# A hybrid RWKV-7/gMLP layer on one core: the inverse's substitution given out in 15 portions, its turning pinned, and the transposing of token rows made a stream of its own

## The chip, the cores and the metric

The kernel runs as one program on one core of a Trainium2 chip. The metric is the time of an execution in microseconds (us) on the device. The engines named below are TensorE (PE, matrix products), VectorE (DVE), ScalarE (ACT), GpSimd (POOL) and SyncE (SP, which here only issues DMA transfers). Each engine works through its own instructions strictly in the order in which they stand in the program.

## The reference

One layer on 576 tokens (64 of a running stream, 512 of a new one), 1024 channels, everything in fp32. What matters here:

```python
p   = rms_norm(x) @ w_in                 # columns: RWKV r|k|v|lora, gMLP u|v, gate_A, gate_B
o_a = rwkv7(p)                           # per token t, 16 heads of 64:
#   sa = S a_t ; S = S * w_t + sa b_t^T + v_t k_t^T ; y_t = S r_t       (a = -kk, b = kk * a_rate)
#   out = (group_norm(y) + sum(r * k * r_k) * v) * g                   ("bonus" is the second term)
o_b = gmlp(p)
m   = sigmoid(gate_A) * (o_a @ w_proj_a) + sigmoid(gate_B) * (o_b @ w_proj_b)
x   = x + rms_norm(m @ w_o)
x   = x + rms_norm((silu(f @ w_gate) * (f @ w_up)) @ w_down)           # f = rms_norm(x)
```

## The kernel before, in words

**Layout.** Activations lie with channels on the 128 partitions and tokens along the free axis (128 x 576, worked in two halves of 288). A weight block of 128 columns is loaded (`raw`, two buffers), split into a rounded high part on ACT (`whi`, line 303) and the rest on POOL (`wlo`, line 306), and used in three products per k-step (line 287, helper `mmul`). A block of `w_in` is 2 halves x 8 k-steps x 3 = 48 products `pj` of 128x288.

**The middle stage** (about 100 to 640 us of the span) is the time mixing. It goes over 8 pairs of heads (`hp_`), each in the chunked form: 9 chunks of 64 tokens. Its parts are Python generators ("streams") that record instructions:

- `elementwise`: the decay products `z` (four, line 287), `sg`, the running sum `L` (a DVE scan, line 671), the exponentials `EL` and `sg<-L` (lines 675 and 677), the square `q<-k` (line 685) and its column sums `n` on PE, `AR` and `BK`, the in-chunk products `am` and from them `AB` and `AK`. It then goes on in the same generator to transpose token rows (`tb`, `tr`, `tv` on PE; `At`, `Kt`, `Vt` are the copies) and to form `WV`, and last to the bonus (`bo` on PE, then `bonus` on DVE). Event `A` is set after `am`, `tb` and `values` on the way, `elem` at the end, and only after `elem` does the next pair's `elementwise` begin.
- `inverse`: inverts the 64x64 triangular matrices. Its 16x16 diagonal blocks go through DRAM: eight transfers `d_inv<-AB` (line 748), one load `M<-d_inv`, then 15 substitution steps of two DVE instructions each (`Xt<-X,M`, line 853, and `X<-X,Xt`, line 856), then `d_inv<-X` and eight transfers `IV<-d_inv` (line 861). `turn()` is a DVE transposition `IT<-IV` (line 864) that waits for them; PE products `m`, `mp`, `mu` then put the blocks together, with a second `turn()` between.
- `batch`: products `d`, `e`, `c` for all chunks; nine DVE instructions (lines 955 and 956) write `TD` and `AR` from `e`, and two ACT copies write `C` from `c` (line 959); then the products `y`.
- `chain`: the recurrence over chunks. A first pair of products `pc` is followed by two DVE additions `S` and `So` (line 994), then six more times one product `pc` and one addition; each `pc` needs the addition before it. Then `py`.
- `finish`: group norm, `to`, `g`, output to DRAM (`d_oa`).

**What sets the order.** `Weave.run` keeps a planned clock: a stream yields either a planned delay (table `LAT`) or an event with a delay, and while all streams wait, `pj` products of the next weight block are put in. The order in which PE's instructions are recorded is the order in which PE runs them (`manual_schedule`). For the other engines a scheduler orders the instructions of each engine by its own idea of when their inputs are ready, preferring what was recorded earlier; `keep_in_program_order(ins)` pins an instruction behind whatever was recorded last on its engine before it. Before the change the first `Xt` of each inverse is pinned, and all 30 substitution instructions are recorded at one planned instant. The blocks for `r`, `k` and `v` of the next pair are taken out of PSUM only after event `elem` of the pair before (`project(..., after=...)`).

**After the middle stage** come the output products `pa`, `pb`, `po` and the feed-forward `fg`/`pd`, which the diff does not touch. Between the last pair's chain and the first `pa` stand the products `gv`.

## Time and profile before

| | |
|---|---|
| median of 3 runs | 1273.09 us (1272.32 to 1274.91) |
| the profiled execution | 1264.63 us, span 1262.8 us |
| mean granted TensorE clock in it | 0.966 |
| PE busy | 1200.6 us of the span (95%) |
| DVE / ACT / POOL busy | 43% / 37% / 49% |

All views of the profile come from this one execution. Times in a view count from the start of its span. A matmul group's "idle before" is the time that PE stood still just ahead of its instructions, with the instruction that ended that wait. PEclk is the granted share of PE's full clock in a stretch. Since PE is busy for 95% of the span, the time can change mainly through what PE waits for and through its clock.

### The profile page before, as it was taken

The page shows a single profiled execution, that of the slowest core. Times are in us where ns is not written, and L with a number is a line of the kernel's source. Part 1 is how long each engine was busy: PE and PEld are TensorE (multiplying, and loading weights), DVE is VectorE, ACT ScalarE, POOL GpSimd, SP SyncE. Part 2 cuts the span into 40 slices and gives each one's busy share as a digit, 9 for nine tenths or more (in the row PEclk, how much of TensorE's full clock was granted, in tenths as well). Part 3 has the DMA queues.
Part 4 walks back from the last instruction along what each step waited for, and adds up shares of the span by engine and source line. Part 5 has one row for each costly group of instructions (what it writes and reads, how often), then busy time and mean ns, then how long its engine had stood idle before and what let it go on. Part 6 is the DMA issues. An engine that isn't in the chain of part 4 may idle for free.

```text
span 1262.8 us, 29911 instructions
## 1 busy us (share of the span) xinstructions
PE 1200.6 (95%) x12926; PEld 1166.8 (92%) x12926; DVE 539.3 (43%) x1081; ACT 464.4 (37%) x889; POOL 614.8 (49%) x484
## 2 busy tenths in 40 slices
PE   7999999989999899989999999989999999999997
PEld 6989889888898889879999999989999999999996
DVE  5755545663655356533452542464333333300003
ACT  5545253533544353524351223452222222222220
POOL 6656244542445254522353654366565656543442
PEclk9999898998998989889999999989999999999998
DMA  5233221322132212223354543222222222243222
GB/s 180 82 101 98 62 79 50 96 71 67 47 90 66 71 54 73 76 65 90 117 187 131 191 146 111 69 108 87 86 86 92 85 85 84 80 155 92 76 76 75
DMA packets 68276, 118.05 MB, mean 93 GB/s; under 512 B 30832, under 2 KB 36208, under 8 KB 68144
## 3 DMA queue, kind: packets, MB, share of 16 engines
q1 hardware_dynamic: 68000, 116.06, 30.0%
q8 instruction: 101, 1.65, 0.5%
q14 instruction: 31, 0.25, 0.1%
q10 hardware_dynamic: 144, 0.08, 0.0%
HBM read 99.83 MB, written 16.28 MB: 92 GB/s over the span
## 4 chain that ended last, share of the span: by engine, by line
PE 70%; DVE 11%; ACT 5%; issue 5%; DMA 4%; SPq 3%; POOL 2%; DVEq 0%; ACTq 0%; POOLq 0%
PE fg L287 20%; PE po L287 14%; PE pj L287 11%; PE gv L287 5%; PE pb L287 4%; PE pa L287 3%; SPq L861 2%; DVE X L856 1%; DVE Xt L853 1%; POOL wlo L306 1%; PE fp L287 1%; PE z L287 1%; SPq L748 1%; PE n L287 1%; PE am L287 1%
## 5 line engine op out<-in xcount | busy, mean ns | idle before, releaser
L306 POOL TENSOR_TENSOR wlo<-raw,whi 128x512 fp32r<-128x512 f32 (+1 forms) x288 | 397.0, 1400 | 408.7 <-ACT whi L303 377.4
L303 ACT ACTIVATE whi<-raw 128x1024 fp32r<-128x1024 f32 x144 | 150.1, 1046 | 271.6 <-PE fg L287 168.4
L1274 DVE TENSOR_TENSOR rs<-rs,nsq 128x288 f32<-128x288 f32 (+2 forms) x12 | 9.1, 755 | 105.8 <-ACT nsq L1273 105.8
L1342 DVE TENSOR_TENSOR ft<-ft,fg 128x288 f32<-128x288 f32 x40 | 16.4, 451 | 65.1 <-PE fg L287 63.6
L1336 DVE TENSOR_TENSOR fg<-fg,rs 128x288 f32<-128x288 f32 x40 | 16.5, 453 | 60.1 <-PE fg L287 60.0
L789 POOL TENSOR_TENSOR AR<-eye,eC 128x576 f32<-128x576 f32 x8 | 9.4, 1177 | 63.8 <-PE tr L291 63.8
L853 DVE TENSOR_TENSOR Xt<-X,M 80x15 f32<-80x15 f32 (+7 forms) x120 | 31.0, 258 | 20.1 <-DMA M<-d_inv 16.6
L864 DVE STREAM_TRANSPOSE IT<-IV 128x640 f32<-128x640 f32 x16 | 13.5, 845 | 55.0 <-DMA IV<-d_inv 32.0
L1339 DVE SCALAR_TENSOR_TENSOR ft<-ft,fg 128x576 f32<-128x576 f32 (+1 forms) x24 | 28.6, 1190 | 19.0 <-ACT ft L1338 19.0
L1340 POOL TENSOR_TENSOR ft<-ft,rs 128x576 f32<-128x576 f32 (+1 forms) x24 | 31.6, 1319 | 7.1 <-DVE ft L1339 7.1
L994 DVE TENSOR_TENSOR S<-pc,C 128x64 f32<-128x64 f32 x48 | 10.5, 219 | 55.5 <-PE pc L287 55.5
L856 DVE TENSOR_TENSOR X<-X,Xt 80x15 f32<-80x15 f32 (+7 forms) x120 | 32.0, 266 | 3.5
L287 PE MATMUL pc<-S,TD 128*128 128x64 f32 x112 | 21.6, 278 | 9.9 <-DVE So L994 9.9
L287 PEld LDWEIGHTS pc<-S,TD 128*128 128x128 f32 x112 | 19.6, 210 | 11.4 <-DVE So L994 10.8
L431 ACT ACTIVATE st<-pj 128x288 f32<-128x288 f32 x30 | 12.2, 407 | 48.0 <-PE pj L287 47.4
L287 PE MATMUL pj<-h0h,whi 128*128 128x288 f32 x88 | 29.5, 336 | 0.0
L287 PE MATMUL pj<-h2h,whi 128*128 128x288 f32 x88 | 29.1, 331 | 0.0
L287 PE MATMUL pj<-h1h,whi 128*128 128x288 f32 x88 | 29.1, 331 | 0.0
L287 PE MATMUL pj<-h7h,whi 128*128 128x288 f32 x88 | 28.4, 323 | 0.0
L287 PE MATMUL pj<-h3h,whi 128*128 128x288 f32 x88 | 28.4, 323 | 0.0
L287 PE MATMUL pj<-h4h,whi 128*128 128x288 f32 x88 | 28.3, 322 | 0.0
L287 PE MATMUL pj<-h5h,whi 128*128 128x288 f32 x88 | 28.2, 320 | 0.0
(1200 smaller groups left out, 4323.2 us busy)
## 6 DMA issues: line engine op xcount, KB each, us to landing
raw<-in_w_in SPq DMA_DIRECT2D x50, 512.0 KB, 3.7
raw<-in_w_gate SPq DMA_DIRECT2D x22, 512.0 KB, 3.6
raw<-in_w_up SPq DMA_DIRECT2D x22, 512.0 KB, 3.6
raw<-in_w_down SPq DMA_DIRECT2D x16, 512.0 KB, 3.5
raw<-in_w_gv SPq DMA_DIRECT2D x8, 512.0 KB, 3.7
raw<-in_w_proj_a SPq DMA_DIRECT2D x8, 512.0 KB, 4.0
raw<-in_w_proj_b SPq DMA_DIRECT2D x8, 512.0 KB, 3.7
raw<-in_w_o SPq DMA_DIRECT2D x8, 512.0 KB, 3.6
```

Source lines behind the costliest of these rows:

```text
L287: return pe.matmul(out, lhsT, rhs, **kw)
L303: keep(act.activation(hi[:, :cols], raw[:, :cols], ACT.Copy))
L306: keep(pool.tensor_tensor(lo[:, c0:c1], raw[:, c0:c1], f(hi[:, c0:c1]), ALU.subtract))
L748: sp.dma_start(di[0, h, b].rearrange("u s t -> s u t"), AB[r0_:r0_ + SB].rearrange("p j h t -> p (j h) t")[:, :, SB * b:SB * b + SB])
L853: ins = dve.tensor_tensor(t3, X[:, 0:r, s:s + 1].broadcast_to([NU, r, w]), M[:, s:s + 1, s + 1:SB].broadcast_to([NU, r, w]), ALU.mult)
L856: dve.tensor_tensor(X[:, 0:r, s + 1:SB], X[:, 0:r, s + 1:SB], t3, ALU.add)
L861: sp.dma_start(IV[r0_:r0_ + SB, :, SB * b:SB * b + SB], di[1, h, b].rearrange("u s t -> s u t"))
L864: turn = lambda: dve.transpose(IT.rearrange("p c t -> p (c t)"), IV.rearrange("p c t -> p (c t)"))
L1336: keep(dve.tensor_tensor(g[:, HS[h]], pg, rs2[:, HS[h]], ALU.mult))
L1339: keep(dve.scalar_tensor_tensor(t[:, ts], t[:, ts], 1.0, g[:, ts], ALU.add, ALU.mult))
L1340: pool.tensor_tensor(t[:, ts], t[:, ts], rs2[:, ts], ALU.mult)
L1342: dve.tensor_tensor(t[:, HS[h]], t[:, HS[h]], pu, ALU.mult)
```

## The change

1. The substitution's 15 steps are recorded one by one, 0.75 us of planned time apart (`yield LAT["X"]`), where they were recorded at one instant. Only the first `Xt` is pinned, as before.
2. The first `turn()` of each inverse is pinned behind what is recorded on DVE before it. Its planned delays change (`M` 6.5 to 9.0, `U` 23.0 to 11.0).
3. The transposing of token rows and `WV` leave `elementwise` for a stream `turns` of their own, which starts at event `A`. `elementwise` goes straight from `am` to the bonus, so `elem` is set earlier, and the next pair's `z` follow at once. `lora_w` moves to just after `A`. A new wait keeps `elementwise` behind the transposing of the pair before (`tb`), and the `v` block now also waits for `values` of the pair before.
4. `n2` goes from 6.8 to 8.2 in the plan, with own values for the first two pairs.

No instruction is added or removed on any engine; the arithmetic is the same.

```diff
-    "z0": 5.4, ... "n2": 6.8, ... "bo0": 3.5, "bo": 0.4,
+    "z0": 5.4, ... "n2": 8.2, ... "bo0": 3.5, "v": 2.2, "bo": 0.4,
...
-    "M": 6.5, "U": 23.0, ...
+    "M": 9.0, "X": 0.75, "U": 11.0, ...
...
-        after = ("elem", p_ - 1) if p_ > 0 else None
+        after = [("elem", p_ - 1)] + [("values", p_ - 1)] * (name == "v") if p_ > 0 else []
...
 def elementwise(E):
...
         if hp_ > 1:
             yield (("chain", hp_ - 2), 0.0)
+        if hp_ > 0:
+            yield (("tb", hp_ - 1), 0.0)
...
         clk.signal("A", hp_)
+        if hp_ + 1 < NPAIR:
+            lora[hp_ + 1] = lora_w(lraw)
+        if hp_ > 1:
+            yield (("oa", hp_ - 2), 0.0)
+        rk = q2
...            # the bonus, as it stood at the end before
+        yield LAT["bo0"]
+        yield (("v", hp_), LAT["v"])
...
+        clk.signal("elem", hp_)
+
+    def turns(E):
...            # tb, tr, AR<-eye, tv, WV as they stood in elementwise
         clk.signal("values", hp_)
...
 def inverse(E):
...
-        with tc.high_priority(UPR):
-            for s in range(0, SB - 1):
...
+        for s in range(0, SB - 1):
...
             dve.tensor_tensor(X[:, 0:r, s + 1:SB], X[:, 0:r, s + 1:SB], t3, ALU.add)
+            yield LAT["X"]
...
-        turn()
+        tc.keep_in_program_order(turn())
...
+    def turn_all():
+        for p_ in range(NPAIR):
+            yield (("A", p_), 0.0)
+            yield from turns(EV[p_])
```

On DVE, at the chain of the third pair, this is the order before. `TD` and `AR` belong to that pair, `Xt`, `X` and `IT` to the inverse of the fourth, `S` and `So` are the chain's additions:

```order
L853 TENSOR_TENSOR Xt<-X,M 80x15
L955 TENSOR_TENSOR TD<-e,AR 64x4x64 x2
L856 TENSOR_TENSOR X<-X,Xt 80x15
L956 TENSOR_TENSOR AR<-e,AR 128x4x64
L955 TENSOR_TENSOR TD<-e,AR 64x4x64 x2
L956 TENSOR_TENSOR AR<-e,AR 128x4x64
L955 TENSOR_TENSOR TD<-c,AR 64x64 x2
L956 TENSOR_TENSOR AR<-c,AR 128x64
L864 STREAM_TRANSPOSE IT<-IV 128x640
L994 TENSOR_TENSOR S<-pc,C 128x64
L994 TENSOR_TENSOR So<-pc,C 128x64
```

The 30 instructions of the substitution stand ahead of `TD` here (all but one), and the transposition that waits for the DMA stands ahead of the chain's first additions. The order at the same chain in the changed kernel:

```order
L862 TENSOR_TENSOR Xt<-X,M 80x55
L865 TENSOR_TENSOR X<-X,Xt 80x11x5
L862 TENSOR_TENSOR Xt<-X,M 80x48
L1004 TENSOR_TENSOR S<-pc,C 128x64
L1004 TENSOR_TENSOR So<-pc,C 128x64
L865 TENSOR_TENSOR X<-X,Xt 80x12x4
L862 TENSOR_TENSOR Xt<-X,M 80x39
L865 TENSOR_TENSOR X<-X,Xt 80x13x3
L862 TENSOR_TENSOR Xt<-X,M 80x28
```

The transposition is gone from this place (it stands further down, behind the next pair's `k`), all nine `TD`/`AR` instructions now come before the substitution, and 23 of its 30 instructions stand between them and `S`, seven behind `So`.

On ACT, ahead of the fifth pair's square `q<-k` (for which the products `n` wait), the order before:

```order
L667 ACTIVATE sg<-z,half 128x288 x2
L669 ACTIVATE sg<-sg,chalf 128x576
L667 ACTIVATE ta<-z,half 128x288
L897 ACTIVATE PT<-mp 32x320 x2
L667 ACTIVATE ta<-z,half 128x288
L675 ACTIVATE EL<-L 128x9x64
L677 ACTIVATE sg<-L 128x576
L1036 ACTIVATE oo<-to,vec 128x448
L687 ACTIVATE aq<-ta,nkk 128x576
L485 ACTIVATE shc<-pj 128x1
L486 ACTIVATE q<-pj,vec 128x288
L1036 ACTIVATE oo<-to,vec 128x128
```

and in the changed kernel:

```order
L487 ACTIVATE q<-first 128x2
L843 ACTIVATE WV<-wv 128x512
L844 ACTIVATE WV<-wv 128x128
L484 ACTIVATE shc<-pj 128x1
L485 ACTIVATE q<-pj,vec 128x288
L1031 ACTIVATE gq<-Y 128x640
```

The square comes right behind the last row of each. What waits for the `z` products and the scan `L` stood just ahead of it and is now some 150 `pj` products earlier on PE: between the last `z` and `n` of pairs 2 to 8 stood 30, 12, 33, 12, 27, 15 and 27 products, and now stand 147, 162, 144, 141, 165, 162 and 144.

## The prediction

> **What bounds the kernel now.** I read the page's head first, then the same busy times by stage, then PE's waits.

> ```profile
> span 1262.8 us, 29911 instructions
> PE 1200.6 (95%) x12926; PEld 1166.8 (92%) x12926; DVE 539.3 (43%) x1081; ACT 464.4 (37%) x889; POOL 614.8 (49%) x484
> ```

> ```profile
> 0.00:100.00 100.00, 86.55 (x678) 83.80 (x680) 66.78 (x98) 53.80 (x107) 62.12 (x62) 0.98 0.38 120
> 100.00:640.00 540.00, 504.65 (x7673) 479.15 (x7670) 272.37 (x648) 229.98 (x519) 227.70 (x175) 0.94 0.26 78
> 640.00:1263.00 623.00, 609.41 (x4583) 603.85 (x4581) 200.11 (x336) 180.58 (x264) 325.02 (x248) 0.99 0.33 103
> ```

> PE is the bound. In the middle stage it stands still for 540 - 504.65 = 35.35 us, and its clock is 0.94 there (first figure after POOL's). The change touches this stage alone. Both losses have places. The waits:

> ```profile
> PE n L287 <- ACT q L685: 13.6, 7, 3.1
> PE pc L287 <- DVE So L994: 9.9, 3, 4.0
> PE pc L287 <- ACT C L959: 8.8, 4, 3.5
> PE z L287 <- DVE bonus L834: 3.8, 3, 1.5
> ```

> These are almost all of it (the longest wait for `q`, 3.1 us, belongs to the first pair, ahead of 100 us; small ones make up 2.3 us in sum). The clock, by windows laid on its slow spells:

> ```profile
> 148.80:159.00 10.20, 9.51 (x107) 9.17 (x108) 1.42 (x5) 1.66 (x5) 0.00 (x0) 0.50 0.30 71
> 326.30:329.70 3.40, 3.40 (x16) 3.40 (x15) 2.67 (x7) 0.95 (x2) 2.47 (x2) 0.50 0.01 2
> 558.40:565.20 6.80, 5.71 (x24) 5.71 (x25) 1.48 (x5) 0.00 (x0) 0.00 (x0) 0.50 0.17 61
> sum 64.60, PE 59.29 PEld 57.18 DVE 20.54 ACT 11.78 POOL 16.36; mean PE 6.59 PEld 6.35 DVE 2.28 ACT 1.31 POOL 1.82
> ```

> Nine spells, 64.6 us, at half clock: worth 32.3 us. So the stage loses about 35 + 32 = 67 us, and that is all there is to win.

> **The change, part by part.**

> *The wait of `n`.* The fifth pair before:

> ```profile
> 317.17 0.30 PE L287 MATMUL z<-dwr,lwh 128*128 128x288 f32 x1
> 319.06 2.19 DVE L671 TENSOR_TENSOR_SCAN L<-rmask,sg 128x576 f32<-128x576 f32 x1 [1.88 <-ACT sg L669]
> 321.29 0.69 ACT L675 ACTIVATE EL<-L 128x576 f32<-128x576 f32 x1
> 324.59 0.78 ACT L685 ACTIVATE q<-k,vec 128x576 f32<-128x576 f32 x1
> 325.42 1.53 PE L287 MATMUL n<-cst,q 128*128 128x2 f32 x10 [2.06 <-ACT q L685]
> ```

> The second `z` leads to the scan, the scan to `EL`, and in ACT's order the square `q` stands behind these. 8.25 us pass from that `z` to `n`, with 15 `pj` products and a few small ones between the last `z` and `n`. The change puts 141 to 165 `pj` there, at least 141 x 0.13 us = 18 us. The wait goes for pairs 2 to 8: 13.6 - 3.1 = 10.5 us. What is late next is `k` alone, and it has 8.2 us of plan where its copies, DVE step and square take about 2.5 us. The first pair's `n` stands where it stood; I leave its 3.1 us.

> *The wait of `z`* for `bonus` is for a PSUM bank. `bo` and `bonus` move ahead of `TD` on DVE, with nothing that waits for a DMA before them. I count the 3.8 us as gone.

> *The transposition.* The third pair's chain before:

> ```profile
> 281.60 0.23 DVE L956 TENSOR_TENSOR AR<-c,AR 128x64 f32<-128x64 f32 x1
> 288.60 0.84 DVE L864 STREAM_TRANSPOSE IT<-IV 128x640 f32<-128x640 f32 x1 [6.77 <-DMA X<-in_cst]
> 289.37 0.18 DVE L994 TENSOR_TENSOR S<-pc,C 128x64 f32<-128x64 f32 x1
> 282.41 0.69 PE L287 MATMUL pc<-C,TD 128*128 128x64 f32 x2 [3.51 <-ACT C L959]
> 289.74 0.69 PE L287 MATMUL pc<-S,TD 128*128 128x64 f32 x2 [2.32 <-DVE So L994]
> ```

> DVE stands idle for 6.77 us in front of a transposition whose DMA has not landed, and the addition queued behind it holds PE's second `pc` for 2.32 us. Ahead of that the burst of 30 had held `TD`, and so `C` and the first `pc`, for 3.51 us. With the new order both reasons go in the first, third, fifth and seventh chains: 9.9 + 8.8 = 18.7 us.

> *What comes instead.* At seven of the eight chains 11 to 23 substitution instructions now stand between `TD` and the first `S`, and up to 13 before the next. In five chains the scan `L` of the next pair stands among them, in two ahead of `TD`. PE's second `pc` waits for all of it. The price is bounded by

> ```profile
> L853 DVE TENSOR_TENSOR Xt<-X,M 80x15 f32<-80x15 f32 (+7 forms) x120 | 31.0, 258 | 20.1 <-DMA M<-d_inv 16.6
> L856 DVE TENSOR_TENSOR X<-X,Xt 80x15 f32<-80x15 f32 (+7 forms) x120 | 32.0, 266 | 3.5
> ```

> ```profile
> 274.09 0.22 DVE L853 TENSOR_TENSOR Xt<-X,M 80x60 f32<-80x60 f32 x1
> 274.34 1.17 DVE L856 TENSOR_TENSOR X<-X,Xt 80x60 f32<-80x60 f32 x1
> 274.17 2.51 POOL L306 TENSOR_TENSOR wlo<-raw,whi 128x512 fp32r<-128x512 f32 x2 [6.23 <-ACT whi L303]
> L671 DVE TENSOR_TENSOR_SCAN L<-rmask,sg x8: 1345/2185/2460, 67.1 to 514.2; 128x576 f32<-128x576 f32 x8
> ```

> An undisturbed one takes 0.22 us, 0.24 with the gap behind it; one that meets POOL's `wlo` 1.17. The mean, 0.26 + 0.03, is 0.29 us. The scan takes 1.35 to 2.46 us. How much time PE gives is seen at the last chain, which has no substitution beside it:

> ```profile
> 600.87 1.10 PE L287 MATMUL e<-AB,At 64*64 64x128 f32 x32
> 602.00 0.86 DVE L955 TENSOR_TENSOR TD<-e,AR 64x256 f32<-64x256 f32 x2 [6.22 <-PE e L287]
> 604.88 0.23 DVE L956 TENSOR_TENSOR AR<-c,AR 128x64 f32<-128x64 f32 x1
> 606.84 0.33 PE L287 MATMUL pc<-C,TD 128*128 128x64 f32 x2
> 609.45 0.33 PE L287 MATMUL pc<-S,TD 128*128 128x64 f32 x2
> 611.48 0.33 PE L287 MATMUL pc<-S,TD 128*128 128x64 f32 x2
> ```

> Counted from the start of `e`: `TD`/`AR` end at 4.2, first `pc` at 6.0, second at 8.6, third at 10.6. For a chain with n instructions and s scans ahead of `S` the second `pc` can start at 4.2 + 0.29 n + 2.2 s + 0.5 (the two additions and the way to PE). Where the scan stands ahead of `TD`, I put `TD`'s end at 5.9 and PE 0.5 later. The same sum gives the third `pc` from the instructions between `So` and the next `S`. The eight chains, with the wait at the second and third `pc` together:

> | chain | ahead of S | before next S | wait at mean price |
> |---|---|---|---|
> | 1 | 17, scan | 13 | 5.1 |
> | 2 | 13 | 10, scan | 3.4 |
> | 3 | 23 (scan before TD) | 7 | 4.6 |
> | 4 | 18 (scan before TD) | 12 | 4.7 |
> | 5 | 12, scan | 12 | 3.5 |
> | 6 | 20 | 10, scan | 5.2 |
> | 7 | 21 | 9 | 3.0 |
> | 8 | 0 | 0 | 0 |

> For chain 1: 4.2 + 17 x 0.29 + 2.2 + 0.5 = 11.8, against 8.6, so 3.2; then 13 x 0.29 + 0.35 = 4.1 against 2.05 to the third, so 2.0 more. The sum is 29.5 us. With the undisturbed 0.24 and 1.4 us for a scan the same table gives 15.3 us. I take 22: POOL's row above shows only two `wlo` near a burst, and in the new order not every chain has them there.

> *Portions.* They cost nothing by themselves, since no instruction is added. The inverse ends some 5 us later against the chain than before. That is covered: about 7 us lay between the burst's end (beside `AR<-c` above) and its transposition, and from the chain's start to the inverse's products `m` PE's order has about 28 us of work, of which the substitution takes 14.

> *Transposing as a stream.* `tb` stays among the `pc`, where every second pair had it already. The `M` load must land before `TD` ends:

> ```profile
> 260.28 1.29 DVE L741 TENSOR_TENSOR AB<-am,rmul 128x512 f32<-128x512 f32 x2 [1.27 <-PE am L287]
> 269.78 0.17 DVE L853 TENSOR_TENSOR Xt<-X,M 80x15 f32<-80x15 f32 x1 [3.23 <-DMA M<-d_inv]
> ```

> It took 9.5 us from `AB`. From `am` to `e` there are now at least 57 `pj` (7.6 us) and about 4 us of small products, and `TD` ends 4.2 us later: some 6 us to spare.

> *The end of the stage.* The last chain ends about 60 `gv` products later in PE's order, so these cover less of what the first `pa` needs. Before, `pa` began 30.9 us after `py` and waited 0.47 us; now about 23:

> ```profile
> 652.49 0.54 PE L287 MATMUL pa<-m0h,whi 128*128 128x288 f32 x2 [0.47 <-ACT s L449]
> ```

> Its first seven inputs need a load and seven splits of about 1 us. I take nothing, with up to 3 us in the range.

> **The sum.** Idle in the stage: 35.35 - 10.5 - 3.8 - 18.7 leaves the 2.3 us of small waits; with 22 and 3 for something unseen it is 27, so 8 us less. Clock: each of the nine spells followed a wait of 1.5 us or more and lasted 7.2 us on average. Of the seven new places I let six have one: 43 us at half clock, 21.5 lost instead of 32.3, so 11 us less. Together 19 us: 1264.63 becomes about 1246 for a profiled execution. The median of the runs lies 8.5 us above that execution, so I set 1273.1 - 19 = 1254.

> **Rivals.**

> *Short waits leave the clock alone* (17 in 100). The new waits are mostly split in two of 1 to 3 us. Of the old ones the wait of 2.06 us ahead of 325.42 was followed by half clock from 326.3, which speaks against; three waits of `z` of up to 1.5 us had none, which speaks for. If none of the seven places throttles, all 32.3 us come back: 1273 - 8 - 32 = 1233. [...]

> *The wait has only moved* (7 in 100). At the dear price, 29.5 us, with all seven places throttled for 10 us (35 us lost): 29.5 + 2.3 + 3 + 35 = 70 against 67: no change, 1273.

> *Slower: the substitution begins late* (15 in 100). `S` stands behind 11 or more substitution instructions in a fixed order, so if `M` lands after `TD`, PE waits for the DMA as well. SP's order speaks for it: in three pairs a weight load, which must wait for its buffer, now stands between the eight `d_inv<-AB` and `M`. The 6 us to spare speak against. It decides from about 2 us late at every chain: (3.1 + 2.2 + 4) x 7 is the 65 us lost before. At 3.5 us late, (3.1 + 3.5 + 4.5) x 7 + 2.3 = 80, which is 13 us slower: 1286.

> *The forecast itself*, 1242 to 1266, has 55 in 100; the last 6 lie between it and no change, where only part of the old waits go.

> **How the numbers follow.** About 0.2% (2.5 us) is what a measurement of this kernel can tell from no change. Faster: 55 + 17 + 6 = 0.78; same 0.07; slower 0.15. The range from 1230 (the first rival with a little more) to 1274 (no change) leaves out the slower case and a little of the others.

> **What would show it.** Right: no row of PE `n` waiting for `q` except once, none of `pc` for `C` above 1 us; instead `pc` waiting for `S` or `So` at seven chains, 2 to 5 us each, with DVE busy with `X` and `Xt` up to it; the transposition's idle time (55.0 us before) mostly gone; the stage's clock at 0.95 to 0.97. Wrong: an `Xt` that waits for `M` behind `TD`; `pj` waiting for `wlo`; an idle PE ahead of `pa`.

## The result and the profile after

| | before | after |
|---|---|---|
| median | 1272.70 us (1267.95 to 1274.91) | 1236.91 us (1235.94 to 1239.04) |
| ratio | | 0.9726 [0.9695, 0.9757] |
| profiled execution | 1264.63 us, span 1262.8 us | 1237.70 us, span 1235.9 us |

The change makes the kernel 35.8 us faster; about 19 were forecast (1254, range 1230 to 1274). The head of the profile after, and the middle stage as it was shown of before (columns: length, busy time and instructions of PE, PEld, DVE, ACT, POOL, then the granted clock, the DMA share, GB/s):

```profile
span 1235.9 us, 29949 instructions
PE 1187.6 (96%) x12926; PEld 1154.5 (93%) x12926; DVE 547.8 (44%) x1081; ACT 466.1 (38%) x889; POOL 614.1 (50%) x484
...
100.00:640.00 540.00, 518.78 (x7913) 493.66 (x7913) 294.31 (x685) 240.14 (x527) 243.76 (x189) 0.98 0.30 86
```

PE's idle time in the whole span fell from 1262.8 - 1200.6 = 62.2 to 1235.9 - 1187.6 = 48.3 us, so 13.9 less; the middle stage alone gave 14.1 (35.35 to 21.22). The other 13.0 us are PE's busy time for the same 12926 products, and two things of opposite sign are in it. The products `fg` of the feed-forward, which the diff does not touch, took longer after the change. All 1920 of them in the stretch where they stand, before and then after (busy time of PE, PEld, DVE, ACT):

```profile
858.60:1109.50 250.90, 250.43 (x1920) 249.77 (x1920) 59.64 (x103) 14.62 (x22) 1.00 0.27 83
```

```profile
824.70:1082.30 257.60, 256.64 (x1920) 256.02 (x1920) 59.81 (x103) 14.62 (x22) 1.00 0.27 81
```

The granted clock is 1.00 in both. All 13 profiles other than that of before show 256.6 to 256.7 us, also the two of the kernel before with one small edit far from `fg`. So the profiled execution of before was 6.2 us short there, for a reason that stays open, and the change did not lengthen `fg`. All other products together took 13.0 + 6.2 = 19.2 us less, because less time passes at half clock: in the spells of the middle stage PE was busy for 59.3 us before (the sum row in the prediction) and for 19.3 after (the sum row below), and half of the 40.0 us between them is 20.0. 13.9 + 19.2 - 6.2 makes the 26.9 us between the two profiled executions. The waits of PE that bear on the change (sum, times, longest, in us):

```profile
PE pc L286 <- DVE So L1004: 10.8, 6, 3.5
...
PE gv L286 <- POOL wlo L305: 3.3, 2, 2.7
PE n L286 <- ACT q L684: 3.1, 1, 3.1
PE pc L286 <- DVE S L1004: 2.3, 4, 1.2
PE am L286 <- ACT oo L1046: 2.2, 2, 1.4
...
PE mp L286 <- DVE IT L874: 0.8, 1, 0.8
```

The waits for `C`, for `bonus` and of `n` (but for the first pair) are gone, and what waits now is `pc` behind the substitution: 13.1 us. Windows laid on the spells of half clock in the middle stage:

```profile
275.00:281.85 6.85, 6.26 (x26) 6.25 (x27) 2.08 (x13) 0.00 (x0) 0.00 (x0) 0.50 0.17 33
305.75:309.15 3.40, 3.40 (x93) 3.08 (x92) 2.22 (x4) 1.18 (x4) 1.71 (x2) 0.50 0.46 137
462.75:466.17 3.42, 3.42 (x16) 3.22 (x15) 2.36 (x12) 2.89 (x7) 0.19 (x1) 0.50 0.65 173
524.20:527.60 3.40, 3.40 (x18) 3.40 (x16) 1.21 (x7) 0.41 (x1) 0.00 (x0) 0.50 0.13 34
602.70:606.10 3.40, 2.80 (x15) 2.40 (x13) 2.40 (x3) 0.38 (x1) 3.40 (x3) 0.50 0.38 94
sum 20.47, PE 19.28 PEld 18.35 DVE 10.27 ACT 4.86 POOL 5.30; mean PE 3.86 PEld 3.67 DVE 2.05 ACT 0.97 POOL 1.06
```

Five spells of 20.5 us, where nine had lasted 64.6.

### The profile page after: what moved, and what is told of

Read it like the earlier page. It is cut to its first block, busy times and chain, and to the rows that moved or that the text cites. A ratio compares the mean times of both kernels' runs of the same rounds, so it can differ in the third digit from the quotient of the medians.

```text
span 1235.9 us, 29949 instructions
## 1 busy us (share of the span) xinstructions
PE 1187.6 (96%) x12926; PEld 1154.5 (93%) x12926; DVE 547.8 (44%) x1081; ACT 466.1 (38%) x889; POOL 614.1 (50%) x484
## 3 DMA queue, kind: packets, MB, share of 16 engines
q1 hardware_dynamic: 68000, 116.06, 30.9%
## 4 chain that ended last, share of the span: by engine, by line
PE 76%; DVE 13%; ACT 3%; issue 3%; POOL 3%; DMA 2%; SPq 0%; DVEq 0%; POOLq 0%; ACTq 0%
PE fg L286 20%; PE pj L286 16%; PE po L286 15%; PE pb L286 4%; PE gv L286 4%; PE pa L286 3%; POOL wlo L305 2%; DVE X L865 2%; DVE Xt L862 2%; PE am L286 2%; PE z L286 1%; PE d L286 1%; DVE TD L965 1%; PE pc L286 1%; DVE y L1324 1%
## 5 line engine op out<-in xcount | busy, mean ns | idle before, releaser
L286 PE MATMUL pc<-S,TD 128*128 128x64 f32 x112 | 20.9, 270 | 13.1 <-DVE So L1004 10.8
L286 PEld LDWEIGHTS pc<-S,TD 128*128 128x128 f32 x112 | 18.3, 198 | 15.6 <-DVE So L1004 12.2
L865 DVE TENSOR_TENSOR X<-X,Xt 80x15 f32<-80x15 f32 (+7 forms) x120 | 29.4, 245 | 3.9
L1035 POOL TENSOR_TENSOR gm<-gm,mhalf 128x10 f32<-128x10 f32 x8 | 16.2, 2022 | 27.3 <-DVE gm L1034 27.2
L1004 DVE TENSOR_TENSOR S<-pc,C 128x64 f32<-128x64 f32 x48 | 10.5, 219 | 42.8 <-PE pc L286 42.8
L765 POOL TENSOR_TENSOR BK<-BK,EL 128x576 f32<-128x576 f32 x16 | 19.8, 1238 | 16.9 <-PE am L286 16.9
L286 PE MATMUL pj<-h6h,whi 128*128 128x288 f32 x88 | 28.1, 320 | 0.0
```

Source lines behind the costliest of these rows:

```text
L286: return pe.matmul(out, lhsT, rhs, **kw)
L765: pool.tensor_tensor(by_chunk(BK[:, x, :]), by_chunk(BK[:, x, :]), EL[:, :, 64:65].broadcast_to([P, NCH, 64]), ALU.mult)
L865: dve.tensor_tensor(X[:, 0:r, s + 1:SB], X[:, 0:r, s + 1:SB], t3, ALU.add)
L1035: pool.tensor_tensor(m, m, mhalf, ALU.pow)
```

## Experiments

Every kernel was timed against the one before (medians 1272.3 to 1274.3 us in these rounds, single executions 1266.9 to 1278.8), but for the three with added waits, which have a single execution. A profile shows one execution: that of before lies 8.1 us below its median, that of M 6.5 lies 6.8 above, the others within 3.3. "Stage" is 100 to 640 us of the profiled execution, half clock by the records of the clock.

| kernel | median us | ratio | stage: PE idle, half clock |
|---|---|---|---|
| before | 1272.7 | | 35.4, 64.9 |
| before, turning pinned | 1247.8 | 0.9812 [0.9761, 0.9863] | 23.9, 41.0 |
| before, M 9.0 | 1257.2 | 0.9876 [0.9835, 0.9916] | 36.7, 30.7 |
| after | 1236.9 | 0.9726 [0.9695, 0.9757] | 21.2, 20.5 |
| after, no pin | 1239.5 | 0.9743 [0.9699, 0.9787] | 23.5, 20.5 |
| after, no portions | 1241.1 | 0.9756 [0.9715, 0.9796] | 24.4, 13.7 |
| after, no stream | 1257.7 | 0.9884 [0.9839, 0.9930] | 31.4, 44.4 |
| after, M 6.5 | 1239.4 | 0.9740 [0.9704, 0.9776] | 23.8, 27.3 |
| after, all 30 pinned | 1219.7 | 0.9577 [0.9532, 0.9622] | 10.8, 6.8 |
| the same, two small edits | 1223.1 | 0.9607 [0.9569, 0.9645] | 14.6, 20.5 |
| the same, one small edit | 1220.1 | 0.9583 [0.9550, 0.9615] | 10.2, 10.2 |

### One part at a time

The theory of the first four (W) was the prediction's: the gain is made of waits that go, and the rest of the loss stands behind the substitution.

**The pin alone**, in the kernel before:

```diff
-        turn()
+        tc.keep_in_program_order(turn())
```

> The kernel before with the first transposition of each inverse pinned behind what is recorded ahead of it on DVE, nothing else. Theory W (each wait of PE costs its length, and half of a slow-clock spell behind it if it is longer than about 1.5 us): the transposition leaves its place ahead of S and So at four chains and ahead of the bonus at three pairs, so the waits of pc for So (9.9 us) and of z for bonus (3.8 us) go and some 14 us of half clock with them; those of n for q and of pc for C stay. 13.7 + 7 = about 20 us less than before: 1253 us. Rival S (the stream of its own is what pays, and DVE only waits elsewhere): within 5 us of the kernel before, 1268 to 1273.

Measured: 1247.84 us. The rows of PE's waits that answer to those of the kernel before:

```profile
PE pc L287 <- ACT C L959: 10.2, 4, 4.8
PE n L287 <- ACT q L685: 9.7, 4, 3.1
```

The waits for `So` behind the transposition (9.9 us) and for `bonus` are gone, the one for `C` stays. Theory W holds for these and for the time, but the wait of `n` fell as well, from 13.6 to 9.7 us, where W had it stay. One line gives about two thirds of the gain (24.5 of 35.8 us).

**The change without its pin:**

```diff
-        tc.keep_in_program_order(turn())
+        turn()
```

> The changed kernel with the transposition's pin taken away. In its order the transposition now stands among the chain's last additions, ahead of AB and the last S or So at six chains. Theory W: the DMA lands some 22 us after e, DVE gets there at 16 to 18, so PE waits 3 to 4 us at six or seven chains, with a spell of 3.4 to 6.8 us of half clock each: 25 + 12, so 1265 to 1275 us. Rival S: no more than 5 us over the changed kernel, 1242 us or less.

Measured: 1239.52 us, a miss for W and in rival S's range. The transposition does stand idle again in front of its DMA, but `S` is no longer behind it at most chains:

```profile
PE pc L286 <- DVE So L1004: 10.7, 6, 3.5
...
PE pc L286 <- DVE S L1004: 5.6, 7, 1.9
```

```profile
L874 DVE STREAM_TRANSPOSE IT<-IV 128x640 f32<-128x640 f32 x16 | 13.4, 840 | 32.6 <-DMA IV<-d_inv 18.1 <-ACT IV L896 14.6
```

The second row is DVE's (busy, mean ns, idle before): 18.1 us of waiting for the DMA, of which PE pays 3.3 (5.6 against 2.3 for `S`), at the ends of three chains. So the pin is worth much where it stands alone and 2.6 us here, which the intervals do not separate from nothing: with the substitution behind `TD`, the scheduler puts the transposition behind the first additions by itself.

**The change without its portions** (all 30 recorded at once, as much planned time behind them):

```diff
-            yield LAT["X"]
...
-        yield lat("U", hp_)
+        yield 15 * LAT["X"] + lat("U", hp_)
```

> The changed kernel with the substitution's 30 instructions recorded at one planned instant, the same planned time in all. In the scheduler's order 11 to 20 of them stand ahead of S in seven chains, none in one chain (11 to 23 with portions). Theory W: the same waits within 3 us, so 1234 to 1241 us: the portions as given out are worth nothing. Rival P (the portions pay): S waits for most of the 30, about 3 us more at each of seven chains with clock, 1255 us or more.

Measured: 1241.09 us, at the upper end of what W had. The portions as they are given out are worth some 4 us, which the intervals do not separate from nothing: only the first of the 30 is pinned, and the scheduler put 12 to 20 of them ahead of `S` in six chains here, and 12 to 23 in seven chains of the changed kernel.

**The change without its stream** (`turns` called from `elementwise` where the code stood before):

> The changed kernel with the transposing and WV back in the elementwise stream ahead of the bonus, so that the next pair's z come late again (12 to 36 products pj between the last z and n). Theory W: n waits again for the square, about 1.5 us at seven pairs since it is planned 1.4 us later than before, each with a spell of half clock: 10 + 12 us, 1255 to 1262 us. Rival T (pin and portions were the whole gain): within 4 us of the changed kernel.

Measured: 1257.65 us, in W's range, but not for its reason. `n` waits only for the first pair, as in the changed kernel; what came back is other:

```profile
PE am L286 <- DVE AR L721: 4.8, 2, 2.4
...
PE m L286 <- ACT aq L686: 3.3, 2, 1.7
...
PE z L286 <- POOL lwl L647: 2.0, 2, 1.0
```

`n2`, the planned time ahead of `n`, stays at 8.2 here and is the likely reason, but no run changed it alone. The time that the stream had given to `am`, `m` and `z` is missed. The stream is worth about 20 us in the changed kernel: its removal costs the most of the three parts.

### What makes the order at the chains

The plan's number `M` sets when the substitution is recorded. In the kernel before, 9.0 in place of 6.5 alone puts all of it behind `TD` (13 to 20 of its instructions ahead of the first `S` in four chains, none ahead of it in three), and the transposition behind the first additions.

```diff
-    "M": 6.5, "U": 23.0,
+    "M": 9.0, "U": 23.0,
```

> The kernel before with a single number of the plan changed: M 9.0 in place of 6.5. That alone puts the substitution behind TD on VectorE in all seven chains (13 to 20 of its instructions ahead of S) and the transposition behind the chain's first additions, while no stream, no portions and no pin are added. Theory M (the gain at the chains comes from this order, whatever makes it): the pc waits for C (8.8 us) and for So behind the DMA (9.9) go, waits of 1 to 4 us for S or So come, about 12 us in sum, the n waits stay: 1252 to 1262. Rival (the order needs the stream or the portions): within 5 us of 1272.

Measured: 1257.24 us, as forecast, though 12 us of waits for `S` and `So` had been expected and 18.0 came, and the waits of `n` fell (13.6 to 8.2). How is the surprise:

```profile
PE pc L287 <- DVE S L994: 13.0, 8, 2.5
PE n L287 <- ACT q L685: 8.2, 5, 3.3
...
PE pc L287 <- DVE So L994: 5.0, 3, 2.5
...
100.00:640.00 540.00, 503.31 (x7756) 477.94 (x7757) 294.41 (x670) 234.97 (x528) 237.23 (x183) 0.97 0.29 83
```

The stage stands idle for 36.7 us, not less than before (35.4). 18.0 us of waits for `S` and `So` have taken the place of 18.7 for `C` and `So`, but in eleven pieces of at most 2.5 us, not seven of up to 4. The clock is 0.97 in place of 0.94, with 30.7 us at half clock in place of 64.9, and PE's busy time in the whole span is 8.6 us less (1192.0 against 1200.6), or 14.8 without `fg`. So shorter waits of about the same sum are the gain, as far as one pair of profiles can show: with the 6.2 us of `fg` these two differ by 12.8 us, the medians by 15.4.

The opposite, the changed kernel with `M` 6.5:

> The changed kernel with M back at 6.5: 12 to 30 substitution instructions stand ahead of or among the nine TD and AR instructions again, pin, portions and stream stay. Theory M: the first pc waits for C at most chains, about 2 us each, 15 us in place of the 13 us for S and So, and nearly every one of these waits fills a clock window, so the stage loses another 5 to 10 us: 1243 to 1255. Rival (only the pin and the stream count): 1234 to 1240.

Measured: 1239.44 us, so theory M falls and the rival stands. In the profile, an execution of 1246.23 us, `pc` waits 5.2 us for `C` and 2.2 for `So`, less than the 13.1 of the changed kernel; small waits elsewhere (`am`, `z`) make it up. With pin and stream there, it makes no measurable difference on which side of `TD` the substitution stands.

### All 30 pinned

```diff
-            if s == 0:
-                tc.keep_in_program_order(ins)
-            dve.tensor_tensor(X[:, 0:r, s + 1:SB], X[:, 0:r, s + 1:SB], t3, ALU.add)
+            tc.keep_in_program_order(ins)
+            tc.keep_in_program_order(dve.tensor_tensor(X[:, 0:r, s + 1:SB], X[:, 0:r, s + 1:SB], t3, ALU.add))
```

Now the portions stand where they are recorded, 8 ahead of `S` (10 in one chain).

> The changed kernel with all 30 substitution instructions of an inverse pinned where they are recorded, so that 8 of them stand ahead of S instead of 11 to 23, and 2 to 4 between the later additions. Theory W (what is left of the loss stands behind the substitution): the 13.1 us that PE waits for S and So in the changed kernel fall to at most 3 us, and the half clock behind four of these waits (17 us, worth 8.5) goes with them: 1237 - 10 - 8 = 1219, within 1214 to 1226. Rival T (the substitution only ends later and holds up the inverse: IT, m, mp or the next chain wait instead): 1233 to 1242.

Measured: 1219.65 us, 17 us below the changed kernel; rival T falls. The third chain in the changed kernel, DVE and then PE:

```profile
267.59 0.23 DVE L966 TENSOR_TENSOR AR<-c,AR 128x64 f32<-128x64 f32 x1
...
269.74 1.27 DVE L865 TENSOR_TENSOR X<-X,Xt 80x55 f32<-80x55 f32 x1
271.04 1.20 DVE L862 TENSOR_TENSOR Xt<-X,M 80x60 f32<-80x60 f32 x1
...
275.32 0.21 DVE L1004 TENSOR_TENSOR So<-pc,C 128x64 f32<-128x64 f32 x1
...
275.59 0.69 PE L286 MATMUL pc<-S,TD 128*128 128x64 f32 x2 [3.53 <-DVE So L1004]
```

and with all 30 pinned:

```profile
265.11 0.23 DVE L965 TENSOR_TENSOR AR<-c,AR 128x64 f32<-128x64 f32 x1
...
267.16 0.22 DVE L1003 TENSOR_TENSOR S<-pc,C 128x64 f32<-128x64 f32 x1 [0.17 <-ACT whi L302]
...
267.43 1.10 DVE L862 TENSOR_TENSOR Xt<-X,M 80x55 f32<-80x55 f32 x1
268.57 1.20 DVE L864 TENSOR_TENSOR X<-X,Xt 80x55 f32<-80x55 f32 x1
...
269.42 0.33 PE L286 MATMUL pc<-S,TD 128*128 128x64 f32 x2
...
PE pc L286 <- DVE S L1003: 2.3, 2, 1.8
...
100.00:640.00 540.00, 529.18 (x8038) 504.61 (x8037) 313.34 (x703) 241.60 (x528) 252.22 (x195) 0.99 0.31 92
```

The two instructions that meet POOL's `wlo` (1.10 and 1.20 us in place of 0.2) now run while PE is busy with other products, and the second `pc` does not wait. This is the kernel that beats both.

**Two small edits on top** (the first pair's `n2` at 13.0; the splits of the attention output pinned, `m*l`, so that `gm` stands ahead of `m0l`):

```diff
-    "n2@0": 10.5,
+    "n2@0": 13.0,
...
-            eng.tensor_tensor(lo, src, f(hi), ALU.subtract)
+            keep(eng.tensor_tensor(lo, src, f(hi), ALU.subtract))
```

> As the kernel with all 30 pinned, and two small edits more: the first pair's square sums come later in the plan (n2@0 13.0), and the splitting of the attention output's low parts is pinned, so that gm stands ahead of m0l on VectorE. Theory W: n's 3.1 us and gv's 3.3 us go, with two half-clock spells of 3.4 us (1.7 us each): 10 us below the kernel with all 30 pinned, 1205 to 1216. Rival: what these two waits covered (the load and split behind n, the second product of gv) waits instead, and it is within 3 us of the kernel with all 30 pinned.

Measured: 1223.05 us, 3.4 us above the kernel with all 30 pinned, so W falls and the rival is nearly met. `n` waits 1.1 us in place of 3.1 and the wait of `gv` is gone, but the `pj` products that were put ahead of `n` are missing at the other end: from the last `py` to the first `pa` it is 23.6 us in place of 28.3, and

```profile
PE pa L286 <- ACT s L448: 5.0, 1, 5.0
```

**The second of these edits alone:**

> The kernel with all 30 substitution instructions pinned and only the second of the two small edits: the splitting of the attention output's low parts is pinned, so that VectorE's gm stands ahead of m0l. PE's order is the same. Theory: the 3.0 us that gv waits for wlo go, with a spell of 3.4 us (1.7 us), and the cover ahead of pa stays as it was, since the other edit moved pj products away from there: 1215 with 1212 to 1218 as its range. Rival (the 5.0 us at pa in the kernel with both edits came from this one): 1219 to 1224.

Measured: 1220.08 us: no change, in the rival's range but not by its reason, since `pa` waits 0.5 as before. The theory had the wrong engine:

```profile
577.07 0.69 ACT L346 ACTIVATE m1h<-gin 128x576 fp32r<-128x576 f32 x1 [0.89 <-DMA gin<-d_oa]
577.66 0.72 ACT L1030 ACTIVATE gq<-Y 128x640 f32<-128x640 f32 x1
...
579.52 2.43 POOL L1034 TENSOR_TENSOR gm<-gm,mhalf 128x10 f32<-128x10 f32 x1 [10.89 <-DVE gm L1033]
```

`gm` now comes first on DVE, but its input `gq` stands on ACT behind `m1h`, which waits for a load; so POOL, with the `wlo` that `gv` needs queued behind its own `gm`, gains little. `gv` waits 2.7 us in place of 3.0. So this pin alone does not take the wait of `gv` away, as the kernel with both edits did.

### Which waits bring half clock

The kernel with all 30 pinned has almost no waits at the chains. 8, 10, ... 22 DVE additions ahead of the first `S` of chain 1, 2, ... 8 give them back in doses:

```diff
+            if n == 0:
+                dz = rp.tile([P, HD], F32, tag="dz", name="dz")
+                for _ in range((8, 10, 12, 14, 16, 18, 20, 22)[hp_]):
+                    tc.keep_in_program_order(dve.tensor_tensor(dz, pc[:, 0], add(2), ALU.add))
```

> As the kernel with all 30 pinned, with 8, 10, 12 ... 22 further VectorE additions of 128x64 (about 0.23 us each, their result unused) pinned ahead of the first S of chain 1, 2, ... 8, which gives the second pc of each chain a wait that grows by some 0.45 us from chain to chain, from about 0 to 3 us (less in the last, which has no substitution beside it). Theory L (length decides): chains with a wait under 1.5 us show full clock behind it, those with more than 2.2 us a spell of 3.4 or 6.8 us at half clock, so three or four spells, all in the later chains; time 1228 to 1238. [...]

> The same additions in the opposite order, 22 ahead of the first chain's S and 8 ahead of the eighth's. Theory L: the waits fall from about 3 us to 0, and the spells stand behind the first three or four chains now, none in the later ones. Rival P: the spells stay at the chains where the ascending order had them.

Measured: 1253.1 and 1251.5 us, where theory L had 1228 to 1238 for the first. The doses came out larger than planned, because the additions read `pc` and begin only behind it, and uneven, because a scan and `wlo` fall among them: 0.8, 3.1, 1.0, 2.0, 2.8, 4.4, 3.9, 3.9 us in the ascending order and 4.4, 5.1, 2.5, 2.5, 2.3, 2.8, 1.3, 0.3 in the other. Spells follow the 2nd and the 5th to 8th in the first kernel and the 1st to 4th and the 6th in the second. So the place does not decide (rival P falls), and five waits of 2.5 to 3.1 us were followed by spells. But length alone does not decide either: 2.3 us had no spell, and 1.7 us at an `am` had one.

The records of the clock tell more. All its recorded changes in an execution lie whole multiples of 3.413 us apart (24 records before and 16 after, each within 0.003 us of this grid). So I cut each of the 14 profiles (before, after and the twelve experiments) into windows of that length on this grid, and counted, for windows at full clock from 25 us on, PE's idle time in the window and whether the next one was at half clock:

```
PE idle in the window    windows   next at half clock
under 0.9 us                4584          9
0.9 to 1.2                    45          6
1.2 to 1.5                    49         14
1.5 to 1.85                   27         12
1.85 and more                 81         81
```

The bounds of the rows were chosen with the counts in view.

The same kernel once more should then have the same waits and, where the border lies elsewhere, other spells.

> The kernel with 8 to 22 added VectorE instructions in ascending order, once more. Reading of the runs so far: the clock is decided in windows of 3.413 us that run freely against the program; a window in which PE stands still for 1.9 us or more is followed by one at half clock, one with less than 1.2 us is not. Then in this execution the waits are the same as in the first one to 0.2 us, but the windows lie elsewhere: a wait of 1.5 to 3 us that falls across a border brings no spell, and every window with over 1.9 us idle is followed by half clock. Rival (a wait's length or its place alone decides): the spells stand behind the same waits as in the first execution.

Measured: 1251.52 us. The borders lay only 0.2 us later, but the program was 0.6 us earlier at the fourth chain, which shows it. Its wait, first and second execution, and the two windows around each:

```profile
336.46 0.43 PE L286 MATMUL pc<-S,TD 128*128 128x64 f32 x2 [1.97 <-DVE So L1007]
...
332.18:335.59 3.41, 2.32 (x84) 2.01 (x83) 2.97 (x14) 2.88 (x7) 0.00 (x0) 1.00 0.02 5
335.59:339.00 3.41, 2.54 (x20) 2.54 (x21) 2.09 (x12) 1.22 (x2) 0.00 (x0) 1.00 0.04 10
```

```profile
335.89 0.69 PE L286 MATMUL pc<-S,TD 128*128 128x64 f32 x2 [1.97 <-DVE So L1007]
...
332.41:335.82 3.41, 1.51 (x50) 1.22 (x42) 3.00 (x16) 2.11 (x5) 0.00 (x0) 1.00 0.00 0
335.82:339.23 3.41, 3.34 (x14) 3.34 (x15) 1.35 (x8) 1.07 (x2) 0.00 (x0) 0.50 0.04 10
```

The same 1.97 us: split over a border, 1.09 us idle in one window and 0.87 in the next, the clock stays at 1.00; within one window, 1.9 us idle, the next is at 0.50. The other seven chains had their spells, or none, where they had had them.

One half of the expectation failed: a window with less than 1.2 us idle should bring no spell, and 15 in the table did, one of them in this execution (0.34 us idle, half clock from 301.7). Nine of the 15 are the row under 0.9 us. All nine windows hold nine or ten of a pair's ten products `n`, of two columns each, and 40 to 80 of the products `m` or `mp`, of 16 or 32 columns: PE counts as busy there with very small products. In the changed kernel such a window runs from 302.3 to 305.7. With all 30 pinned the same products and the same wait of 0.34 us are cut by a border at 294.2, and no spell follows (the changed kernel first):

```profile
302.06 1.17 PE L286 MATMUL n<-cst,q 128*128 128x2 f32 x10
303.57 0.85 PE L286 MATMUL m<-IT,AB 16*32 16x16 f32 x80 [0.34 <-DVE IT L874]
```

```profile
292.98 1.17 PE L286 MATMUL n<-cst,q 128*128 128x2 f32 x10
294.49 0.85 PE L286 MATMUL m<-IT,AB 16*32 16x16 f32 x80 [0.34 <-DVE IT L873]
```

If the time of `n`, `m`, `mp` and `mu` is counted as idle, half clock follows none of the 4539 windows under 1.2 us, 30 of 155 from 1.2 to 2.0, and 92 of 92 from 2.0 on. This fits the 14 profiles better, but no run was made to test it.

## Why the prediction was right, and where its sizes were off

1236.9 us lies within the range, but below the 1242 to 1266 that was called the forecast itself; the range reached down to 1230 only to take in the first rival. So the mechanism was right, and that the time is inside is in part luck. Both gains came out larger: 14 us of idle time for 8, and 19 us of clock for 11, so 33 in place of 19 (the medians differ by 35.8).

- **The wait of `n`** and **the wait of `z`**: both went, as predicted. 3.1 us of the first pair are left of 13.6, and no row of `z` for `bonus`. But the reason given for `n`, the 141 to 165 products put ahead of it, is not needed: without the stream only 12 to 36 stand there, and `n` waited no more than with it.
- **The transposition.** The rows for `C` are gone, and DVE's idle time ahead of `IT` fell from 55.0 us to 15.0, none of it for a DMA:

```profile
L874 DVE STREAM_TRANSPOSE IT<-IV 128x640 f32<-128x640 f32 x16 | 13.3, 834 | 15.0 <-ACT IV L896 15.0
```

- **What comes instead**: the mechanism was right, the term too large, 22 us against 13.1 measured, below even the cheap end of 15.3. By chains: 1.3, 1.8, 3.5, 1.3, 0.2, 2.3, 2.6 and 0. The second `pc` waited 10.8 us in all, where the prediction's rule gives about 15.6 at the mean price, and the third 2.3, where it gives about 13.7. (By that rule chains 3 and 4 come to 4.3 each, not to 4.6 and 4.7; and the five chains with a scan among the instructions are four, in its table and in the trace.) In the first, 17 substitution instructions and the scan took

```profile
145.32 0.16 DVE L862 TENSOR_TENSOR Xt<-X,M 80x15 f32<-80x15 f32 x1
...
149.01 1.35 DVE L670 TENSOR_TENSOR_SCAN L<-rmask,sg 128x576 f32<-128x576 f32 x1
...
150.79 0.43 PE L286 MATMUL pc<-S,TD 128*128 128x64 f32 x2 [0.72 <-DVE So L1004]
```

  5.1 us from the first to `S` at 150.39, where 17 x 0.29 + 2.2 = 7.1 had been set. Three sizes failed. The mean of 0.29 us was put on every chain, though POOL's `wlo` fell into four of the seven (2, 3, 6 and 7) and the others ran at 0.22 to 0.24. The scan, at a median of 2.2 us before, took 1.35 in seven cases of eight. And what PE itself needs from the second `pc` to the third was set at 2.05 us, from the last chain: it was 2.4 to 2.5 in chains 1, 2, 4 and 5, and 3.5 to 4.2 in chains 3, 6 and 7, where PE was at half clock after its first wait.
- **Portions** cost nothing: right; as given out they bring next to nothing either.
- **Transposing as a stream, the end of the stage**: no `Xt` waited for `M` behind `TD`, `pa` waits 0.47 us as before. From the first of the last `py` to `pa` it is 29.1 us, where about 23 were forecast and 30.9 had been. The slower rival did not come.
- **Unseen**: 3 us were set aside; `gv` 3.3, `am` 2.2 and `mp` 0.8 make 6.3. The stage's idle time is 21.2 us against 27 forecast, so 14 less and not 8.
- **The clock**: this step failed as it was put, "six of seven places have a spell", 43 us. 20.5 us came, and the stage's clock is 0.98, not 0.95 to 0.97. Of the five spells three follow chain waits of 3.5, 2.3 and 2.6 us, one the 2.7 us of `gv`, and one (305.75) a wait of 0.3 us together with the small products `n` and `m`; the chains with 0 to 1.2 us at a time have none. The rival "short waits leave the clock alone" (1233) was the nearer one in time, but its condition failed too, since three of the seven chains had a spell. 47.4 us less at half clock in the whole span took 19.2 us from PE's busy time without `fg`, 0.41 us for each, where 0.5 was reckoned and 11 us forecast. (The three dose kernels against the one with all 30 pinned give 0.50, 0.59 and 0.57: 13.5 us for 27.2, 10.9 for 18.3 and 12.6 for 22.0, with the spells from 25 us on.)
- **The baseline.** The profiled executions differ by 26.9 us, the medians by 35.8. The prediction carried its gain over to a median that lay 8.5 us above the profiled execution as if that offset stayed. It did not: after, the profiled one lies 0.8 above its median. 6.2 us of the offset can be laid to the short `fg` of that one execution: its mean clock, 0.966, is no reason, since another execution of the kernel before took 1274.28 us at 0.966. For the rest, executions of the kernel before do differ in clock (1278.81 us at 0.959, 1266.9 at 0.970). That its many waits of 2 to 4 us meet the windows by chance fits this; it was not shown for executions without a trace.

What stays open: why `fg` was 6.2 us shorter in one profiled execution at the same granted clock, and why a microsecond of half clock costs 0.41 us in one pair of profiles and up to 0.59 in others. In both profiles `pj` products began 0.133 us apart at full clock and 0.240 us apart at 0.50 (medians). From these two an estimate is 0.45 us lost for each microsecond at half clock, so the figures above 0.5 hold something else as well.

## What to carry to other kernels

When a chain on PE needs a short instruction of another engine, count what stands ahead of it in that engine's order, and pin all of a long batch, not its first instruction: here the one pin with portions left the kernel at 1237 us and pins on every portion brought 1220. An order can be worth as much as a mechanism: one number of the plan (1257) or one pin (1248) brought a large part of what the whole change did, the parts do not add up, and each is known only when it has been taken away from both sides. Price waits by their length too: with `M` 9.0, eleven waits of at most 2.5 us came in place of seven of up to 4, and with nearly the same sum (18.0 us for 18.7) the stage had 30.7 us at half clock in place of 64.9 (one pair of profiles showed it).

## What the runs showed of the hardware

In the 14 profiles, 203 of the 295 substitution instructions on DVE that ran beside POOL's `wlo` took 1.0 to 1.32 us, where undisturbed ones take 0.16 to 0.22; 52 kept 0.22 or less. Of the eight scans before, the one with POOL idle took 1.35 us and two that ran wholly beside `wlo` 1.36; two that began 0.30 us behind the start of a `wlo` took 2.18 and 2.19, and three that began 0.05 to 0.06 us behind one, with POOL's `aq<-aq,k` following it, 2.45 to 2.46.
